# MLP down-projection in two passes over 1024 columns, 18 of 64 pairs of k-tiles with Strassen's seven block products

## The chip, the core and the metric

The kernel runs on one core of a Trainium2 chip. TensorE multiplies (its results go to PSUM, in eight banks of 128 x 512 float32 numbers), VectorE (DVE), ScalarE (ACT) and GpSimd (POOL) compute on SBUF, and SyncE (SP) issues most of the transfers from memory. Each engine works off its own instructions in a fixed order, and semaphores tie the engines together. The metric is the device time of one execution in microseconds: before the change a median of 2107.43 us over three runs (2106.3 to 2108.21).

## The reference

A trunk of two layers over 256 tokens of 2048 numbers, all in float32. Layer 0 mixes tokens with a state-space mixer, layer 1 with windowed attention; each is followed by an MLP of width 8192:

```python
def sqrelu_mlp(h, w_up, w_down):
    return jnp.square(jax.nn.relu(h @ w_up)) @ w_down
...
        h = h + sqrelu_mlp(rms_norm(h, mlp_norm[i]), mlp_w_up[i], mlp_w_down[i])
```

The change concerns the second product: 256 tokens x 8192 times 8192 x 2048, once per layer.

## The kernel before

Every float32 number that TensorE multiplies is split into a high part (`hi`, rounded to TensorE's fast format by a cast on ScalarE, line 667) and a low part (`lo`, the rest, by a subtract on VectorE, line 668). A product is then three matmuls: high x high, low x high, high x low.

Weights stream through three rings of buffers of 128 x 2048: `raw` (two buffers, loaded from memory on SP's queue, line 662), `hi` (three) and `lo` (three). `wnext` hands out the oldest loaded block and lets `wload` load one ahead. A raw buffer is free again when its subtract is done, a high or low buffer when the last matmul that reads it is done.

`mlp` first does the up-projection: 64 blocks of 128 hidden units, each with 16 matmuls of 512 columns (line 827) and 16 of 256 columns (line 829); the input lies in `act`, high and low part side by side. `up_post` adds, rectifies, scales and squares into `hT`, which holds all 8192 hidden units of the 256 tokens in float32.

Then comes the down-projection, 64 k-tiles of 128 hidden units. `split(kt)` (lines 871 and 872) makes the high and low part of that k-tile's activations, 256 columns, in a pool of three buffers that lies apart from `act`. `down` then does, for each of two token tiles, three runs of four matmuls of 512 columns (line 879): the four column blocks follow each other with the same stationary operand, and all eight banks collect over the whole 64 k-tiles. That is 24 matmuls per k-tile, 1536 per MLP. The last two k-tiles are held back and done bank by bank, so that `end` (line 909) adds each finished bank to the residual while TensorE goes on. After the first MLP `end` also prepares the next norm (a multiply on GpSimd, line 704, and squares on ScalarE, line 706); after the second it sends the output.

What order the instructions have on each engine is set by a scheduler when the program is built: it goes by dependences, by the order of the code and by its own timing model, and may move an instruction far ahead where its buffers allow it.

## Time and profile before

| what | us |
|---|---|
| median of three runs | 2107.43 |
| the profiled execution | 2104.89 |
| its span in the trace | 2103.1 |
| first down-projection, first to last matmul, from 752.5 | 348 |
| second down-projection, from 1750.9 | 348.2 |

The profile describes one execution. A row of a group names a line of the kernel, the engine, the operation, the operands (output, arrow, inputs), and then how many there were, their busy time together, and the mean of one in ns. A row of the timeline begins with the start and the length in us; rows of equal instructions are merged, with their count behind the x. The chain of waits follows the work that ended last back from the end. PE is TensorE's matmul, PEld its load of the stationary operand.

### The profile page before, as it was taken

Reading aid. Unit: us, or ns where it says so; the run is one execution under the profiler, and the core shown is the slowest. Engines: PE = TensorE matmul, PEld = TensorE weight load, DVE = VectorE, ACT = ScalarE, POOL = GpSimd, SP = SyncE. Lnnn points to the kernel's source line nnn. Section 1 sums busy time; section 2 is a strip of 40 time slices with the busy share of each in tenths; the row PEclk is TensorE's granted clock in tenths of the full one; section 3 lists DMA queues with packets and bytes.
Section 4 is the critical chain, followed back from the end, with each engine's and each line's share of the span. In section 5 each row is a group of like instructions: output and inputs, shape, how many; then the busy total and the mean of one; then the engine's idle time right before and its main releaser. Section 6 shows DMA issues by size and latency. Waiting matters only on the chain. (4 is left out here: it accounts for less than half of the span.)

```text
span 2103.1 us, 33054 instructions
## 1 busy us (share of the span) xinstructions
PE 2029.9 (97%) x13844; PEld 1712.2 (81%) x13844; DVE 1245.2 (59%) x1824; ACT 979.8 (47%) x1238; POOL 330.1 (16%) x248
## 2 busy tenths in 40 slices
PE   4989999899999999999999889999999999999999
PEld 4877778788888888888888667788888888888887
DVE  8899736755555554444556877565555555444444
ACT  5553645544444444344444556544444444443442
POOL 5988721200000000000012430100000000000000
PEclk9999999999999999999999999999999999999999
DMA  3224455455555555655554332455555555555554
GB/s 119 69 98 144 151 196 195 177 187 196 182 197 182 193 187 194 208 197 196 194 178 170 121 121 81 150 189 201 191 185 196 182 197 182 200 187 193 200 187 153
DMA packets 59685, 364.28 MB, mean 173 GB/s; under 512 B 6816, under 2 KB 9152, under 8 KB 19600
## 3 DMA queue, kind: packets, MB, share of 16 engines
q1 hardware_dynamic: 54144, 342.32, 46.4%
q10 hardware_dynamic: 5184, 19.49, 2.8%
q8 instruction: 108, 1.77, 0.3%
q14 instruction: 41, 0.34, 0.0%
q0 software_dynamic: 208, 0.36, 0.0%
HBM read 360.05 MB, written 2.10 MB: 172 GB/s over the span
## 5 line engine op out<-in xcount | busy, mean ns | idle before, releaser
L668 DVE TENSOR_TENSOR slot<-slot,slot 128x2048 fp32r<-128x2048 f32 (+1 forms) x321 | 714.6, 2229 | 737.3 <-ACT slot L667 730.2
L667 ACT CAST slot<-slot 128x2048 fp32r<-128x2048 f32 (+2 forms) x357 | 623.0, 1751 | 731.0 <-PE bank L879 377.7
L879 PE MATMUL bank<-slot,slot 128*128 128x512 f32 x3072 | 696.7, 389 | 0.0
L879 PEld LDWEIGHTS bank<-slot,slot 128*128 128x128 f32 x3072 | 576.6, 188 | 119.4
L827 PE MATMUL bank<-slot,slot 128*128 128x512 f32 x2048 | 492.0, 392 | 3.1 <-DVE ms L724 1.7
L827 PEld LDWEIGHTS bank<-slot,slot 128*128 128x128 f32 x2048 | 376.8, 189 | 76.6 <-DVE slot L716 2.1
L829 PEld LDWEIGHTS bank<-slot,slot 128*128 128x128 f32 x2048 | 263.1, 191 | 10.3
L829 PE MATMUL bank<-slot,slot 128*128 128x256 f32 x2048 | 266.2, 283 | 0.0
L686 PE MATMUL bank<-slot,slot 128*128 128x512 f32 x544 | 218.6, 403 | 6.2 <-ACT slot L667 4.9
L687 PE MATMUL bank<-slot,slot 128*128 128x512 f32 x544 | 214.9, 395 | 0.0
L688 PE MATMUL bank<-slot,slot 128*128 128x512 f32 x544 | 208.6, 396 | 6.3 <-POOL slot L668 6.1
L837 ACT ACTIVATE slot<-slot 128x256 f32<-128x256 f32 x128 | 52.9, 415 | 164.1 <-DVE slot L836 164.1
L686 PEld LDWEIGHTS bank<-slot,slot 128*128 128x128 f32 x544 | 103.5, 190 | 30.9 <-ACT slot L667 6.1
L688 PEld LDWEIGHTS bank<-slot,slot 128*128 128x128 f32 x544 | 102.0, 189 | 30.0 <-POOL slot L668 7.6
L687 PEld LDWEIGHTS bank<-slot,slot 128*128 128x128 f32 x544 | 103.5, 190 | 20.6 <-issue 0.5
L668 POOL TENSOR_TENSOR slot<-slot,slot 128x1024 fp32r<-128x1024 f32 (+2 forms) x36 | 101.1, 2819 | 103.4 <-ACT slot L667 98.2
L950 POOL DMA_DIRECT2D slot<-in_pos x1 | 0.8, 754 | 608.2 <-DVE slot L872 608.2
L532 DVE TENSOR_TENSOR bank<-bank,slot 128x256 f32<-128x256 f32 x126 | 54.4, 431 | 4.1
L836 DVE SCALAR_TENSOR_TENSOR slot<-slot 128x256 f32<-128x256 f32 x128 | 54.2, 425 | 4.2
L872 DVE TENSOR_TENSOR slot<-slot,slot 128x256 fp32r<-128x256 f32 x128 | 53.4, 418 | 4.0 <-ACT slot L871 4.0
L704 POOL TENSOR_TENSOR slot<-slot 128x512 f32<-128x512 f32 x16 | 28.0, 1758 | 172.7 <-DVE slot L1158 62.6
L871 ACT CAST slot<-slot 128x256 fp32r<-128x256 f32 x128 | 51.1, 400 | 7.9 <-PE bank L879 7.9
(217 smaller groups left out, 1390.8 us busy)
## 6 DMA issues: line engine op xcount, KB each, us to landing
slot<-in_wup SPq DMA_DIRECT2D x128, 1024.0 KB, 4.8
slot<-in_wdn SPq DMA_DIRECT2D x128, 1024.0 KB, 4.8
slot<-in_wqkv SPq DMA_DIRECT2D x20, 1024.0 KB, 4.9
slot<-in_wge ACTq DMA_DIRECT2D x32, 512.0 KB, 3.7
slot<-in_wgl SPq DMA_DIRECT2D x16, 1024.0 KB, 5.1
slot<-in_wo SPq DMA_DIRECT2D x16, 1024.0 KB, 5.0
slot<-in_bz SPq DMA_DIRECT2D x16, 336.0 KB, 3.7
slot<-in_cp SPq DMA_DIRECT2D x16, 256.0 KB, 2.6
```

The costliest lines, as they stand in the source:

```text
L532: yield v.tensor_mul(xy, lb, st[:, k - 1].rearrange("p r (o g) -> p r o g", o=1).broadcast_to([P, 2, 2, n]))
L667: self.nc.scalar.copy(hi[:, c], raw[:, c])
L668: (self.nc.gpsimd if e == "g" else self.nc.vector).tensor_sub(lo[:, c], raw[:, c], hi[:, c].bitcast(F32))
L686: pe.matmul(out, lhsT=xh, rhs=wh, start=first, stop=False)
L687: pe.matmul(out, lhsT=xl, rhs=wh, start=False, stop=False)
L688: pe.matmul(out, lhsT=xh, rhs=wl, start=False, stop=last)
L827: pe.matmul(bk, lhsT=wh[:, kt], rhs=act[:, kt].rearrange("p x c -> p (x c)"), start=(kt == 0), stop=False)
L829: pe.matmul(bk[:, :L], lhsT=wl[:, kt], rhs=act[:, kt, 0], start=False, stop=(kt == KT - 1))
L836: nc.vector.scalar_tensor_tensor(s, s, 0.0, rb, op0=ALU.max, op1=ALU.mult)
L837: nc.scalar.activation(hT(fb), s, AF.Square)
L872: nc.vector.tensor_sub(hl, hT(kt), hh.bitcast(F32))
L879: pe.matmul(bks[tt][cb], lhsT=x[:, ts], rhs=w[:, cb * 512:(cb + 1) * 512], start=(kt == 0 and w is wh and x is hh), stop=(kt == NK - 1 and ...
```

## The change

**Layout.** The down-weights are stored anew: a load of 128 x 2048 now holds two k-tiles (256 hidden units) by 1024 output columns, as four blocks of 512 columns in the order B12, B22, B11, B21 (row: which k-tile; column: which half of the 1024). It is still 1 MB, and there are still 64 per MLP.

**Two passes.** The down-projection goes over the 32 pairs of k-tiles twice, each time for 1024 of the 2048 columns. A pass collects in four banks, one for each token tile and column block. `split` now prepares a pair of k-tiles (512 columns), and does so in both passes.

**Strassen.** A plain pair is eight block products (two token tiles, two k-tiles, two column blocks), 24 matmuls. In 9 of the 32 pairs of a pass, every third one, seven products take their place, 21 matmuls (Winograd's form of Strassen's scheme). For these pairs `split` also makes four sums of activation blocks and their high and low parts; `wload_fast` splits three of the weight blocks as they are, then forms differences in place in the raw buffer, and splits all four results. So such a pair takes two high and two low buffers. Four more banks (`p1`, `q5`, `q6`, `q7`) collect over the Strassen pairs of a pass; `fold` adds them to the residual after the last of them.

**Buffers.** For the down-projection each ring gets one buffer more: a raw one at 49664 and a high and a low one in the area of `act`, at 23552 and 25600. The parts of the activations (`aform`) lie in the area of `act` too, at 27648 and 29696. In the first pass Strassen pairs are 2, 5, ... 26, in the second 0, 3, ... 24; with three raw buffers they all use the one at 49664.

**The end.** In the first MLP, the norm's preparation of the first 1024 columns is issued in the second pass already (pair 19).

In the order listings below, `slot_82` is the area of the old raw buffers, `slot_83` that of the new one, `slot_4069` that of the old high buffers, `slot_2733` and `slot_2734` that of the low ones, `slot_4067` (from 23552) that of `act` and now of `aform` and the new high and low buffer, `slot_313`, `slot_4602` and `slot_4603` are `hT`, `slot_7236` held the parts of the activations before, and `slot_79` is a small pool, now with the activation sums too.

First place: VectorE in the middle of the first pass of the first down-projection. Before, from the middle of the same down-projection:

```order
L872 TENSOR_TENSOR slot_7236<-slot_313,slot_7236 128x256
L668 TENSOR_TENSOR slot_2733<-slot_82,slot_4069 128x2048
L872 TENSOR_TENSOR slot_7236<-slot_313,slot_7236 128x256
L668 TENSOR_TENSOR slot_2734<-slot_82,slot_4069 128x2048
L872 TENSOR_TENSOR slot_7236<-slot_313,slot_7236 128x256
```

Now, 12 of the 14 instructions of one period of three pairs (a Strassen pair and two plain ones; the two left out are the first sum, L903, ahead of these rows, and one more low part, L909, behind them):

```order
L688 TENSOR_TENSOR slot_83<-slot_83 128x512
L904 TENSOR_TENSOR slot_79<-slot_79,slot_4602 128x128
L686 TENSOR_TENSOR slot_2734<-slot_83,slot_4069 128x1536
L905 TENSOR_TENSOR slot_79<-slot_79,slot_4602 128x128
L689 TENSOR_TENSOR slot_83<-slot_83 128x512
L690 TENSOR_TENSOR slot_83<-slot_83 128x1024
L672 TENSOR_TENSOR slot_4067<-slot_82,slot_4067 128x2048
L909 TENSOR_TENSOR slot_4067<-slot_313,slot_4067 128x512
L686 TENSOR_TENSOR slot_2734<-slot_83,slot_4069 128x2048
L672 TENSOR_TENSOR slot_2733<-slot_82,slot_4069 128x2048
L909 TENSOR_TENSOR slot_4067<-slot_313,slot_4067 128x512
L909 TENSOR_TENSOR slot_4067<-slot_79,slot_4067 128x512
```

Where a subtract of 2048 and one of 256 columns took turns, six of the 14 instructions now make sums and differences, and all low parts of activations are 512 columns wide. L688 to L690 are the differences of weight blocks, L903 to L905 the sums of activation blocks; the second subtract of the Strassen pair (L686 with 2048 columns), which gives up the raw buffer `slot_83`, stands between the two subtracts of plain pairs.

Second place: VectorE at the seam between the first MLP's up- and down-projection. Before:

```order
L668 TENSOR_TENSOR slot_2734<-slot_82,slot_4069 128x2048
L835 TENSOR_TENSOR slot_79<-bank,slot_79 128x256
L836 SCALAR_TENSOR_TENSOR slot_79<-slot_79 128x256
L668 TENSOR_TENSOR slot_2734<-slot_82,slot_4069 128x2048
L872 TENSOR_TENSOR slot_7236<-slot_313,slot_7236 128x256
L668 TENSOR_TENSOR slot_2733<-slot_82,slot_4069 128x2048
```

Now:

```order
L903 TENSOR_TENSOR slot_79<-slot_313 128x256
L904 TENSOR_TENSOR slot_79<-slot_79,slot_313 128x128
L686 TENSOR_TENSOR slot_2734<-slot_83,slot_4069 128x1536
L905 TENSOR_TENSOR slot_79<-slot_79,slot_313 128x128
L672 TENSOR_TENSOR slot_4067<-slot_82,slot_4067 128x2048
L689 TENSOR_TENSOR slot_83<-slot_83 128x512
L909 TENSOR_TENSOR slot_4067<-slot_313,slot_4067 128x512 x2
L858 TENSOR_TENSOR slot_79<-bank,slot_79 128x256
L909 TENSOR_TENSOR slot_4067<-slot_79,slot_4067 128x512
```

Before, the parts of the first activations (L872, into an area of their own) stood much earlier, among the first blocks of the up-projection. Now the first low part (L909) stands behind the subtracts of two weight blocks (L686, L672) and a difference (L689). At the same seam of the second MLP (`slot_9722` is the new raw buffer there, `slot_11474` is `hT`) it is this:

```order
L903 TENSOR_TENSOR slot_79<-slot_11474 128x256
L904 TENSOR_TENSOR slot_79<-slot_79,slot_11474 128x128
L686 TENSOR_TENSOR slot_2734<-slot_9722,slot_4069 128x1536
L905 TENSOR_TENSOR slot_79<-slot_79,slot_11474 128x128
L909 TENSOR_TENSOR slot_4067<-slot_11474,slot_4067 128x512 x2
L858 TENSOR_TENSOR slot_79<-bank,slot_79 128x256
L689 TENSOR_TENSOR slot_9722<-slot_9722 128x512
L909 TENSOR_TENSOR slot_4067<-slot_79,slot_4067 128x512
```

There no subtract of 2048 columns stands ahead of the first L909.

Third place: SP's queue around the GLU's loads, long ahead of the first MLP. Before:

```order
L562 DMA slot_241<-in_bz 128x672
L662 DMA slot_82<-in_wgl 128x2048 x2
L697 DMA slot_73<-in_gains 128x512 x2
L662 DMA slot_82<-in_wgl 128x2048 x6
L697 DMA slot_73<-in_gains 128x512
```

Now:

```order
L564 DMA slot_241<-in_bz 128x672
L666 DMA slot_82<-in_wgl 128x2048
L679 DMA slot_83<-in_wdn 128x2048
L666 DMA slot_82<-in_wgl 128x2048
L720 DMA slot_73<-in_gains 128x512 x2
L666 DMA slot_82<-in_wgl 128x2048 x6
L720 DMA slot_73<-in_gains 128x512
```

The first load for a Strassen pair stands behind the first GLU load, because its buffer is free so early. On TensorE the two down-projections have 1482 matmuls each where they had 1536; away from them, and from the transposes behind the first, the order of TensorE's instructions is as it was.

The diff, without the lines that only rename:

```diff
+WD = 20 + 16 + 64 + 64
+FAST = (range(2, 27, 3), range(0, 25, 3))
...
+            if len(self.wsrc) in self.wfast:
+                return self.wload_fast(src)
...
+    def wload_fast(self, src):
+
+        v = self.nc.vector
+        raw = self.wr[0].next()
+        self.nc.sync.dma_start(raw, src)
+        b = [raw[:, i * 512:(i + 1) * 512] for i in range(4)]
+        pair = raw[:, 1024:].rearrange("p (x c) -> p x c", x=2)
+        out = []
+        for x, n in (raw[:, 512:], 1536), (raw, 2048):
+            hi, lo = (r.next()[:, :n] for r in self.wr[1:])
+            self.nc.scalar.copy(hi, x)
+            v.tensor_sub(lo, x, hi.bitcast(F32))
+            if n < D:
+                v.tensor_sub(b[0], b[0], b[2])
+                v.tensor_sub(b[1], b[1], b[0])
+                v.tensor_sub(pair, pair, b[1].rearrange("p (o c) -> p o c", o=1).broadcast_to([P, 2, 512]))
+            out += [(hi, lo)]
+        self.wq.append(out)
...
-            t = pool.tile([P, L], F32, name="up_t")
+            t = pool.tile([P, 512], F32, name="u5")
+            t, s = t[:, :L], t[:, L:]
             nc.scalar.copy(t, bk[:, L:])
-            s = pool.tile([P, L], F32, name="up_s")
...
-        def split(kt):
-            hh = pool.tile([P, L], F32R, name="hh", bufs=3)
-            hl = pool.tile([P, L], F32R, name="hl", bufs=3)
-            nc.scalar.copy(hh, hT(kt))
-            nc.vector.tensor_sub(hl, hT(kt), hh.bitcast(F32))
-            return hh, hl
-
-        def down(kt, tt, hh, hl, wh, wl, cbs=range(4)):
-            ts = slice(tt * P, (tt + 1) * P)
-            for x, w in ((hh, wh), (hl, wh), (hh, wl)):
-                for cb in cbs:
-                    pe.matmul(bks[tt][cb], lhsT=x[:, ts], rhs=w[:, cb * 512:(cb + 1) * 512],
-                              start=(kt == 0 and w is wh and x is hh), stop=(kt == NK - 1 and w is wl))
+        def split(kp, fast, tail=False):
+            h = hTs[0][:, 2 * kp:2 * kp + 2] if kp < 16 else hTs[kp // 8 - 1][:, kp % 8 * 2:kp % 8 * 2 + 2]
+            h = h.rearrange("p k c -> p (k c)")
+            a = (atail if tail else aform)[kp % 2]
+            n = a.shape[1] // 2
+            o = [(a[:, :512], a[:, n:n + 512], h)]
+            if fast:
+                s = pool.tile([P, 512], F32, name="u5")
+                q = h.rearrange("p (x c) -> p x c", x=4)
+                t = s.rearrange("p (x c) -> p x c", x=4)
+                v.tensor_add(t[:, 0:2], q[:, 0:4:3], q[:, 1:2].broadcast_to([P, 2, P]))
+                v.tensor_add(t[:, 2], t[:, 1], q[:, 0])
+                v.tensor_add(t[:, 3], t[:, 2], q[:, 2])
+                o.append((a[:, 512:n], a[:, n + 512:], s))
+            for hi, lo, x in o:
+                nc.scalar.copy(hi, x)
+                v.tensor_sub(lo, x, hi.bitcast(F32))
+            return a[:, :n], a[:, n:]
+        def mm(bk, a, j, w, c, stop=False):
+            j, c = slice(j * P, (j + 1) * P), slice(c * 512, (c + 1) * 512)
+            for x, y in ((0, 0), (1, 0), (0, 1)):
+                pe.matmul(bank(bk), lhsT=a[x][:, j], rhs=w[y][:, c], start=bk not in begun, stop=stop and y == 1)
+                begun.add(bk)
...
+        FORMS = (("p1", 0, 0, 1), ("x1", 2, 0, 2), ("x2", 7, 0, 0), ("q5", 5, 1, 0), ("q6", 6, 1, 1), ("q7", 4, 1, 2), ("x3", 3, 1, 3))
+        LATE = FORMS[:1] + FORMS[3:6] + FORMS[1:3] + FORMS[6:]
+
+        def fast(a, w, first, end):
+            for bk, j, g, c in LATE if first else FORMS:
+                mm(bk, a, j, w[g], c, stop=end and bk[0] != "x")
+
+        def plain(a, w, bk, stop=False):
+            t, j = divmod(bk, 2)
+            bk = "x%d" % (bk + 1)
+            for i in range(2):
+                mm(bk, a, 2 * i + t, w, (2, 3)[i] if j == 0 else i, stop=stop and i == 1)
...
+        def fold():
+            c, u, w = (self.tmp.tile([P, 512], F32, name=n) for n in ("hg", "sq", "gain"))
+            nc.scalar.copy(c, bks["p1"])
+            v.tensor_sub(u, bks["q6"], c)
+            v.tensor_add(rs(0, 0), rs(0, 0), c)
+            v.tensor_add(w, u, bks["q5"])
+            v.tensor_sub(rs(0, 1), rs(0, 1), w)
+            v.tensor_add(u, u, bks["q7"])
+            v.tensor_add(rs(1, 0), rs(1, 0), u)
+            v.tensor_add(u, u, bks["q5"])
+            v.tensor_add(rs(1, 1), rs(1, 1), u)
...
+        def end(half, t, j):
+            cb = half * 2 + j
+            cs = slice(cb * 512, (cb + 1) * 512)
+            v.tensor_add(self.resid[:, t, cs], self.resid[:, t, cs], bks["x%d" % (2 * t + j + 1)])
...
-        pend = []
-        for kt in range(NK):
-            hh, hl = nx
-            wh, wl = self.wnext() if kt else w0
-            if kt + 1 < NK:
-                nx = split(kt + 1)
-            if kt == NK // 2 + 4 and not last:
...
+        aform += [ar.get("af#%d" % i, [2048], F32R, at=27648 + 2048 * i) for i in range(2)]
+        more = [ar.get("wx#%d" % at, [2048], dt, at=at) for at, dt in ((49664, F32), (23552, F32R), (25600, F32R))]
+        for r, t in zip(self.wr, more):
+            r.tiles.append(t)
+        nx = split(0, 0 in FAST[0])
+        for half in range(2):
+            bks, begun = {}, set()
+            pend = []
+            for kp in range(NK):
+                a = nx
+                w = self.wnext() if half or kp else w0
+                if half and kp == NK - 4:
+                    for r in self.wr:
+                        r.tiles.pop()
+                        r.i = min(r.i, len(r.tiles) - 1)
+                    ar.free("wx")
+                    atail += [ar.get("at#%d" % i, [1024], F32R, at=49664 + 1024 * i) for i in range(2)]
+                if kp + 1 < NK:
+                    nx = split(kp + 1, kp + 1 in FAST[half], half and kp + 1 >= NK - 2)
+                elif not half:
+                    nx = split(0, 0 in FAST[1])
+                if half and kp == 19 and not last:
+                    ar.free("hT#0")
+                    hx = ar.get("hx", [2, 4, 512], at=31744)
+                    gains = ar.get("hg", [D], at=35840)
+                    nc.sync.dma_start(gains, self.d["gains"][nxt])
+                    self.ss = self.small.tile([P, 2, 4], F32, name="ss")
+                    for t in range(2):
+                        for cb in range(2):
+                            scaled(t, cb)
+                if kp in FAST[half]:
+                    fast(a, w, not begun, kp == FAST[half][-1])
+                    if kp == FAST[half][-1]:
+                        fold()
+                elif kp < NK - 1 - half:
+                    for b in range(4):
+                        plain(a, w, b)
+                else:
+                    pend.append((a, w))
+            if half:
+                ar.free("hT", "af")
+                if not last:
+                    self.act = ar.get("act", [KT, 2, L], F32R, at=23552)
+            n = half and not last
+            for t in range(2):
+                for p in pend[:n]:
+                    for j in range(2):
+                        plain(*p, 2 * t + j)
+                for j in range(2):
+                    for p in pend[n:]:
+                        plain(*p, 2 * t + j, stop=p is pend[-1])
+                    end(half, t, j)
...
+        self.wfast = {n - 1 - 32 * h - kp for n in (64, 64 + WD) for h in range(2) for kp in FAST[h]}
...
-    r["wdn"] = c(mlp_w_down).reshape(2, FF // P, P, D)
+    w = mlp_w_down.reshape(2, FF // P // 2, 2, P, 2, 2, 512).transpose(0, 4, 1, 3, 2, 5, 6).reshape(2, 2, FF // P // 2, P, 4, 512)
+    r["wdn"] = c(w[:, :, :, :, [1, 3, 0, 2]]).reshape(2, FF // P, P, D)
```

51 lines of the change are left out of this document (18 added, 33 removed).

## The prediction

> **What bounds the kernel now.** I read the page first, then the chain of waits, the windows, the groups by form and last the timeline of the down-projection. On the page TensorE is busy for almost the whole span, and the chain of waits that ended last shows the second down-projection as one unbroken piece:
>
> ```profile
> PE 2029.9 (97%) x13844; PEld 1712.2 (81%) x13844; DVE 1245.2 (59%) x1824; ACT 979.8 (47%) x1238; POOL 330.1 (16%) x248
> ...
> 1750.91 348.20 PE bank L879 x1536
> ```
>
> 1536 matmuls in 348.20 us are 226.7 ns each, with no wait between them. The windows view over the first down-projection (columns: length, busy us with instruction counts for PE, PEld, DVE, ACT, POOL, then granted clock, DMA share, GB/s) says what the others have left:
>
> ```profile
> 752.00:1100.00 348.00, 348.00 (x1539) 288.36 (x1539) 174.79 (x166) 143.04 (x137) 7.93 (x9) 1.00 0.56 197
> ```
>
> VectorE works half the time, ScalarE 41%, DMA engines 56%. So a matmul taken away here is worth its 226.7 ns, as long as the operands still arrive in time. The timeline shows the feeding of one k-tile, every 5.44 us:
>
> ```profile
> 898.75 1.91 ACT L667 CAST slot<-slot 128x2048 fp32r<-128x2048 f32 x1 [3.23 <-PE bank L879]
> 900.69 2.29 DVE L668 TENSOR_TENSOR slot<-slot,slot 128x2048 fp32r<-128x2048 f32 x1 [2.81 <-ACT slot L667]
> 902.90 0.42 DVE L872 TENSOR_TENSOR slot<-slot,slot 128x256 fp32r<-128x256 f32 x1
> 903.01 0.33 SPq L662 DMA_DIRECT2D slot<-in_wdn  x1
> ```
>
> The cast waits for TensorE to give up a high tile, the subtract follows 0.03 us behind it, and the next load is issued 0.03 us after the subtract has given up the raw buffer. The L872 subtract starts 0.08 us before the listed end of the one ahead of it: independent VectorE operations overlap by that much.
>
> **What goes.** A plain pair of k-tiles by 1024 columns costs 8 products of 3 matmuls, a Strassen pair 7 of 3. 18 pairs in each of two MLPs remove 18 x 3 x 2 = 108 matmuls: 108 x 0.2267 = **24.5 us**, if the rate stays. One thing could alter the rate: the four column blocks that shared a stationary operand are gone, the stationary changes with each matmul. The up-projection already works so:
>
> ```profile
> 1500.41 3.65 PE bank L827 x16
> ...
> 1501.63 2.43 PE L827 MATMUL bank<-slot,slot 128*128 128x512 f32 x10
> ```
>
> Sixteen from the start of a block take 228.1 ns each, which over 2964 matmuls would cost 4.2 us. But ten from its middle take (2.43 - 0.39) / 9 = 226.7 (0.39 is the last one's own length): the excess belongs to the change from narrow matmuls. I take 0, with 4.2 as the upper end.
>
> **What is added, in steady state.** The pattern repeats every three pairs, one Strassen and two plain: 21 + 24 + 24 = 69 matmuls, 15.64 us. The prices:
>
> ```profile
> L668 DVE TENSOR_TENSOR slot<-slot,slot 128x2048 fp32r<-128x2048 f32 x285 | 654.0, 2295 | 720.8 <-ACT slot L667 715.9 <-PE bank L688 4.9
> L667 ACT CAST slot<-slot 128x2048 fp32r<-128x2048 f32 x293 | 559.5, 1910 | 669.7 <-PE bank L879 377.7 <-PE bank L827 193.7 <-DMA slot<-in_wgl 27.3
> L533 DVE TENSOR_TENSOR slot<-bank,slot 128x128 f32<-128x128 f32 x126 | 36.6, 291 | 4.2
> L872 DVE TENSOR_TENSOR slot<-slot,slot 128x256 fp32r<-128x256 f32 x128 | 53.4, 418 | 4.0 <-ACT slot L871 4.0
> L909 DVE TENSOR_TENSOR slot<-slot,bank 128x512 f32<-128x512 f32 x16 | 10.7, 684 | 8.2 <-PE bank L879 8.1
> L667 ACT CAST slot<-slot 128x512 fp32r<-128x512 f32 x4 | 2.3, 618 | 1.0 <-DVE slot L668 1.0
> ```
>
> Between 256 and 2048 columns a VectorE operation costs 1.05 ns per column, so 1.22 us at 1024 and 1.76 at 1536 are my estimates; a cast of 1536 is 1.48 the same way. VectorE per period: weights of the Strassen pair 1.76 + 2.30, block differences 0.68 + 0.68 + 1.22, activation sums 0.42 + 0.29 + 0.29, their low parts 2 x 0.68; two plain pairs 2 x (2.30 + 0.68). That is **15.0 us** in 14 operations without any overlap, 13.9 with 0.08 each: 89 to 96% of 15.64. ScalarE: 1.48 + 3 x 1.91 + 4 x 0.62 = 9.7. Loads: three, 14.4 us even one after the other (4.8 each, below). So all of it hides, VectorE narrowly. If that cover were gone, the excess over 15.64 would be paid in each of 36 periods.
>
> The narrowest place is the raw buffer that every Strassen pair uses again, three pairs later. Its round: load D, cast 1.48, subtract 1.76, one activation sum 0.29, differences 0.68 and 1.22, then (the second cast runs beside them) a plain subtract 2.30, a low part 0.68 and the second subtract 2.30, as VectorE's order has them. That is D + 10.7, or D + 10.3 with the overlaps. D is read here:
>
> ```profile
> slot<-in_wdn SPq DMA_DIRECT2D x128, 1024.0 KB, 4.8
> DMA to landing us min/median/max: 4.7/4.8/5.5
> ...
> L662 SPq DMA_DIRECT2D slot<-in_wdn x2: 328/328/328, 765.2 to 767.7; - x2
> DMA to landing us min/median/max: 4.7/4.8/4.8
> ...
> L662 SPq DMA_DIRECT2D slot<-in_wgl x2: 328/356/383, 354.6 to 356.9; - x2
> DMA to landing us min/median/max: 7.7/7.8/7.9
> ```
>
> With 4.8 the round is 15.1 to 15.5, inside 15.64 by 0.1 to 0.5 us. In the new order three buffers are released within some 5 us, so loads go out about 2.7 us apart; the pair at 765.2 and 767.7 had that distance and landed in 4.8 all the same. The pair of 7.8 stood behind another load issued 0.4 us ahead. I take D = 4.8 to 5 and no cost.
>
> The fold of the four extra banks (eight VectorE operations, 5.5 us, once per pass) falls on plain pairs, where VectorE needs 3.0 of 5.44 us; its banks are wanted again only after five pairs. Evictions at the end of a pass (0.68 each) are covered by the next pass, which begins with the other four banks: 12 matmuls, 2.7 us. Both 0; uncovered, 5 us a pass. The four early scalings of the first MLP put four GpSimd multiplies beside the subtracts, and those two disturb each other:
>
> ```profile
> L668 DVE TENSOR_TENSOR slot<-slot,slot x321: 1211/2292/5580, 164.9 to 2083.8; 128x2048 fp32r<-128x2048 f32 x143, 128x1024 fp32r<-128x1024 f32 x18
> L668 DVE TENSOR_TENSOR slot<-slot,slot 128x1024 fp32r<-128x1024 f32 x36 | 60.7, 1699 | 16.5 <-ACT slot L667 14.3 <-PE bank L829 2.1
> 1094.23 5.05 POOL L704 TENSOR_TENSOR slot<-slot,slot 128x512 f32<-128x512 f32 x4 [75.31 <-DVE slot L909]
> ```
>
> 1024 columns take 1211 ns alone and 1699 on average in stages with GpSimd at work, 40% more; over 5.05 us that is 2 us late, once. Half of it finds slack: **1.0 us** (0 to 2). The same scalings leave half as much for the tail, worth 0 to 1 us; I take 0.
>
> **What is moved.** One load of down-weights stands on SP's queue between the first two GLU loads:
>
> ```profile
> 255.29 19.18 SPq L662 DMA_DIRECT2D slot<-in_wgl  x2
> 274.64 0.80 SPq L697 DMA_DIRECT2D slot<-in_gains  x2
> 298.94 0.33 SPq L662 DMA_DIRECT2D slot<-in_wgl  x1
> ```
>
> The second GLU load was issued at 274.5, the third only at 298.9; behind the moved load 24 us are free, so 0 (4.8 if they were not). VectorE's first difference goes with it, far ahead of need.
>
> **The start of each down-projection** is a new wait. The activation operands, and a fourth high and low tile, now lie where the up-projection's input was, which is read until its last matmul; before, they lay elsewhere and were ready early. At the seam now:
>
> ```profile
> 750.63 2.08 PE L829 MATMUL bank<-slot,slot 128*128 128x256 f32 x16
> 752.55 5.63 PE L879 MATMUL bank<-slot,slot 128*128 128x512 f32 x24
> ...
> 752.80 2.29 DVE L668 TENSOR_TENSOR slot<-slot,slot 128x2048 fp32r<-128x2048 f32 x1 [2.48 <-ACT slot L667]
> ```
>
> VectorE takes up its next weight tile 0.25 us after the seam. By its new order the first low part stands behind it: in the first MLP 1536 columns, an activation sum, 2048 columns, a difference, then the low part, 1.76 + 0.29 + 2.30 + 0.68 + 0.68 = 5.7; in the second 1.76 + 0.29 + 0.68 = 2.7. Only four matmuls (0.9 us) do without low parts. Idle: 0.25 + 5.7 - 0.9 less overlaps = 4.7, and 1.9: **6.6 us**. Lower end: one cast of 0.62 per MLP, 1.2 in all; upper end 12, if the second goes like the first. Such a gap can also cost clock:
>
> ```profile
> 395.77 1.12 PE L713 MATMUL bank<-ident,slot 128*128 128x128 f32 x4 [3.95 <-POOL slot L704]
> 395.00:400.00 5.00, 4.23 (x14) 3.54 (x15) 4.58 (x18) 1.41 (x4) 2.00 (x2) 0.66 0.33 136
> ...
> 1103.66 0.50 PE L686 MATMUL bank<-slot,slot 128*128 128x512 f32 x1 [1.01 <-ACT slot L716]
> 1098.00:1106.00 8.00, 6.99 (x43) 5.96 (x42) 7.10 (x18) 5.04 (x13) 6.28 (x6) 1.00 0.00 0
> ```
>
> After 3.95 us of idleness the granted clock was 0.66 over 5 us (0.34 x 5 = 1.7 us lost); after 1.01 it stayed 1.00. The first start lies near the longer gap but is cut by four matmuls: 0.8 us, between 0 and 1.7. The Trainium skill ("TensorE: Matmul & The Clock Gate", section "Why this matters for your kernels") says that idle gaps over about 3 us bring the half clock back; the trace agrees, and by that rule alone the first start would cost the full 1.7, a sum later by 0.9.
>
> **Sum.** 24.5 - 6.6 - 1.0 - 0.8 = 16.1 us. The profiled execution took 2104.89 (span 2103.1): 2088.8. The median of the three runs, 2107.43, lies 2.5 above it: **2091 us**.
>
> **Rivals.**
> - The raw buffer's round decides (slower). For it: releases in a bunch, and loads that took 7.8 in bunches. Against it: the pair at 765.2. There are 8 rounds between Strassen pairs in each of 4 passes, 32. The gain is used up when a round takes 15.64 + 16.1 / 32 = 16.1 us, so from D = 5.4 to 5.8 on. With D = 6.3, halfway to 7.8, a round takes 16.6 to 17.0: 1.2 x 32 = 38 us, less 16.1 gained, about 2129 us.
> - VectorE becomes the bound: its waits on its own results keep the operations from overlapping and add some 0.07 us each, 15.0 + 1.0 = 16.0. That is 0.36 x 36 = 13 us given back: 2104 us. For it: the sums and differences depend on each other. Against it: most subtracts are independent.
> - The starts cost only their casts, 1.2, and nothing else is lost: 24.5 - 1.2 = 23.3, 2084 us. For it: TensorE's last up matmuls free parts of that area early. Against it: the order on VectorE.
> - The change not doing what it says is left out: the order has 1482 matmuls in each down-projection for 1536.
>
> **How the numbers follow.** Forecast 0.70, raw buffer 0.10, VectorE bound 0.13, free starts 0.07. The forecast's own bounds (rate up to 4.2, starts 1.2 to 12, scaling, clock) reach from 2084 to 2100. The range goes to 2103.5, up to the VectorE case, and leaves the slower one out: 2084 to 2103.5. A measurement of this kernel tells no less than 0.2%, 4.2 us, from no change. Faster: 0.70 + 0.07 + a little under half of 0.13 = 0.83; same 0.07; slower 0.10.
>
> **What would show it.** 1482 matmuls of the down-projection at 226.7 ns, 336 us, with idle time only in their first 10 us; VectorE about 90% busy while Strassen pairs run; load landings at 4.8 to 5. Wrong, if TensorE waits for VectorE in each period, if the casts of Strassen pairs wait for their load, or if matmuls run at 228 ns.

## The result, and the profile after

The changed kernel takes 2090.7 us (median, 2089.6 to 2094.4), the kernel before 2107.3: a ratio of 0.9924, 95% interval 0.991 to 0.9938, about 16 us less. The prediction was 2091. The profiled execution, the longest of the four, took 2094.37 (span 2092.6).

The page of the changed kernel: 108 matmuls fewer, 22 us less of TensorE, and VectorE up from 59 to 71%.

```profile
PE 2007.8 (96%) x13736; PEld 1692.1 (81%) x13736; DVE 1496.1 (71%) x2144; ACT 1083.2 (52%) x1314; POOL 335.3 (16%) x248
```

Its windows, 100 us in the middle of a first pass (columns as in the prediction). TensorE never stops, VectorE works 90.85 of 100 us:

```profile
800.00:900.00 100.00, 100.00 (x443) 82.79 (x442) 90.85 (x88) 60.72 (x53) 0.00 (x0) 1.00 0.54 198
```

Its chain of waits for the down-projections. Before, one row held all 1536 matmuls; now the first MLP's is in pieces, and the second's is whole from 1753 us on, 335.63 / 1478 = 227.1 ns each with the change of pass and the end in it:

```profile
760.64 231.84 PE bank L915 x1013
1000.92 62.86 PE bank L915 x276
1064.21 4.57 PE bank L915 x20
1070.14 31.78 PE bank L915 x140
...
1753.06 335.63 PE bank L915 x1478
```

What breaks it is seen in the timeline at the first start:

```profile
754.57 1.89 ACT L671 CAST slot<-slot 128x2048 fp32r<-128x2048 f32 x1
...
755.22 1.76 DVE L686 TENSOR_TENSOR slot<-slot,slot 128x1536 fp32r<-128x1536 f32 x1 [0.22 <-PE bank L852]
...
756.36 1.14 ACT L908 CAST slot<-slot 128x512 fp32r<-128x512 f32 x2
...
757.03 1.20 PE L915 MATMUL bank<-slot,slot 128*128 128x512 f32 x4 [1.38 <-ACT slot L908]
757.09 2.29 DVE L672 TENSOR_TENSOR slot<-slot,slot 128x2048 fp32r<-128x2048 f32 x1
...
759.29 0.68 DVE L689 TENSOR_TENSOR slot<-slot 128x512 f32<-128x512 f32 x1
759.90 1.29 DVE L909 TENSOR_TENSOR slot<-slot,slot 128x512 fp32r<-128x512 f32 x2
```

and, by the windows, in the 4 us behind it, at a granted clock of 0.57:

```profile
761.00:765.00 4.00, 4.00 (x12) 3.13 (x11) 4.00 (x11) 0.46 (x2) 0.00 (x0) 0.57 0.61 238
```

Four matmuls start when the first cast (L908) is done, which on ScalarE stands behind the cast of a weight tile (L671); the fifth waits for the first low part (L909), which stands behind a whole weight tile on VectorE, and starts at 760.64. The other place is in the second pass of the first MLP:

```profile
988.50 9.61 POOL L727 TENSOR_TENSOR slot<-slot,slot 128x512 f32<-128x512 f32 x4 [587.52 <-DVE slot L690]
...
988.78 3.17 DVE L672 TENSOR_TENSOR slot<-slot,slot 128x2048 fp32r<-128x2048 f32 x1 [0.40 <-ACT slot L671]
...
991.88 1.78 DVE L909 TENSOR_TENSOR slot<-slot,slot 128x512 fp32r<-128x512 f32 x1
...
993.58 3.38 DVE L686 TENSOR_TENSOR slot<-slot,slot 128x2048 fp32r<-128x2048 f32 x1
...
996.89 3.37 DVE L672 TENSOR_TENSOR slot<-slot,slot 128x2048 fp32r<-128x2048 f32 x1
...
997.02 2.11 PE L915 MATMUL bank<-slot,slot 128*128 128x512 f32 x8 [0.70 <-DVE slot L686]
```

The four GpSimd multiplies of the early scaling take 9.61 us together, and four VectorE operations beside them take 0.88, 1.10, 1.09 and 1.08 us more than their 2.29 and 0.68. One by one, the multiplies took 1.30 us and then, in the timeline:

```profile
989.76 3.35 POOL L727 TENSOR_TENSOR slot<-slot,slot 128x512 f32<-128x512 f32 x1
...
993.07 1.75 POOL L727 TENSOR_TENSOR slot<-slot,slot 128x512 f32<-128x512 f32 x1
...
994.78 3.33 POOL L727 TENSOR_TENSOR slot<-slot,slot 128x512 f32<-128x512 f32 x1
```

Set side by side, the rows show the two engines taking turns. Each of the four VectorE operations ends its usual 2.29 or 0.68 us, less 0.13 to 0.15, behind the end of the multiply that was running when it started. Each of these three multiplies ends 1.15 or 1.16 us behind the end of the VectorE operation that was running. So each waited until the other had all but finished.

I added up, over all matmuls of the down-projections, how much later than 226.6 ns behind the one ahead each starts, leaving out differences under 0.02 us: 0 before, 11.1 us now: 4.1 of waits at the first start and 1.7 of half clock behind it, 3.0 beside the multiplies, 1.5 at the second start, and 0.8 at the changes of pass and the end. 24.5 - 11.1 = 13.4 us, within the interval. The two profiled executions differ by 10.5 us; the other 3 lie ahead of the first down-projection, since the up-projection's last matmul started at 755.4 us here and at 752.4 before, which is scatter as far as the other profiles tell (see the moved load below). This sum, called TensorE's loss below, is what the experiments take apart. Their ratios are to the kernel before, which was timed again beside each of them (medians of 2105.8 to 2106.5 us).

### The profile page after: what moved, and what is told of

Its sections match the earlier page's. It is cut to its first block, busy times and chain, and to the rows that moved or that the text cites. A ratio compares the mean times of both kernels' runs of the same rounds, so it can differ in the third digit from the quotient of the medians.

```text
span 2092.6 us, 33181 instructions
## 1 busy us (share of the span) xinstructions
PE 2007.8 (96%) x13736; PEld 1692.1 (81%) x13736; DVE 1496.1 (71%) x2144; ACT 1083.2 (52%) x1314; POOL 335.3 (16%) x248
## 4 chain that ended last, share of the span: by engine, by line
PE 72%; DVE 5%; DMA 3%; ACT 2%; issue 1%; POOL 0%; SPq 0%; ACTq 0%; DVEq 0%
PE bank L915 32%; PE bank L850 22%; PE bank L852 12%; DVE slot L672 2%; PE bank L709 2%; PE bank L710 1%; PE bank L711 1%; ACT slot L671 1%; DMA slot<-in_wqkv 1%; DMA slot<-in_wo 1%; ACT slot L1136 1%; PE bank L1155 1%; DMA slot<-in_wup 1%; PE bank L1146 1%; DVE slot L1121 0%
## 5 line engine op out<-in xcount | busy, mean ns | idle before, releaser
L672 DVE TENSOR_TENSOR slot<-slot,slot 128x2048 fp32r<-128x2048 f32 (+1 forms) x285 | 633.9, 2227 | 426.6 <-ACT slot L671 423.2
L671 ACT CAST slot<-slot 128x2048 fp32r<-128x2048 f32 (+2 forms) x321 | 554.4, 1733 | 485.2 <-PE bank L850 192.0
L915 PE MATMUL bank<-slot,slot 128*128 128x512 f32 x2136 | 496.2, 390 | 7.4 <-DVE slot L909 5.3
L850 PE MATMUL bank<-slot,slot 128*128 128x512 f32 x2048 | 492.8, 392 | 2.9 <-DVE ms L747 1.5
L915 PEld LDWEIGHTS bank<-slot,slot 128*128 128x128 f32 x2136 | 401.4, 188 | 93.5 <-DVE slot L909 7.4
L850 PEld LDWEIGHTS bank<-slot,slot 128*128 128x128 f32 x2048 | 377.4, 189 | 76.7 <-DVE slot L739 2.1
L852 PEld LDWEIGHTS bank<-slot,slot 128*128 128x128 f32 x2048 | 263.1, 191 | 10.4
L709 PE MATMUL bank<-slot,slot 128*128 128x512 f32 x544 | 217.9, 402 | 6.9 <-ACT slot L671 6.3
L711 PE MATMUL bank<-slot,slot 128*128 128x512 f32 x544 | 208.3, 396 | 7.7 <-POOL slot L672 7.5
L710 PE MATMUL bank<-slot,slot 128*128 128x512 f32 x544 | 214.2, 394 | 0.0
L915 PE MATMUL bank<-slot 128*128 128x512 f32 x828 | 195.8, 389 | 0.0
L915 PEld LDWEIGHTS bank<-slot 128*128 128x128 f32 x828 | 155.3, 188 | 32.3
L686 DVE TENSOR_TENSOR slot<-slot,slot 128x1536 fp32r<-128x1536 f32 x72 | 146.7, 2037 | 19.0 <-ACT slot L685 18.2
L685 ACT CAST slot<-slot 128x1536 fp32r<-128x1536 f32 x72 | 122.3, 1698 | 41.7 <-DMA slot<-in_wdn 28.3
L908 ACT CAST slot<-slot 128x512 fp32r<-128x512 f32 x164 | 97.5, 616 | 82.9 <-PE bank L915 78.4
L709 PEld LDWEIGHTS bank<-slot,slot 128*128 128x128 f32 x544 | 103.2, 190 | 31.0 <-ACT slot L671 7.5
L711 PEld LDWEIGHTS bank<-slot,slot 128*128 128x128 f32 x544 | 101.9, 189 | 31.4 <-POOL slot L672 9.4
L909 DVE TENSOR_TENSOR slot<-slot,slot 128x512 fp32r<-128x512 f32 x164 | 110.7, 693 | 15.7 <-ACT slot L908 15.7
L710 PEld LDWEIGHTS bank<-slot,slot 128*128 128x128 f32 x544 | 103.3, 190 | 20.7 <-issue 0.7
L672 POOL TENSOR_TENSOR slot<-slot,slot 128x1024 fp32r<-128x1024 f32 (+2 forms) x36 | 100.5, 2803 | 104.6 <-ACT slot L671 100.9
```

What stands on the lines that cost most here:

```text
L671: self.nc.scalar.copy(hi[:, c], raw[:, c])
L672: (self.nc.gpsimd if e == "g" else self.nc.vector).tensor_sub(lo[:, c], raw[:, c], hi[:, c].bitcast(F32))
L685: self.nc.scalar.copy(hi, x)
L686: v.tensor_sub(lo, x, hi.bitcast(F32))
L709: pe.matmul(out, lhsT=xh, rhs=wh, start=first, stop=False)
L710: pe.matmul(out, lhsT=xl, rhs=wh, start=False, stop=False)
```

## Experiments

**Two passes without Strassen pairs.**

```diff
-FAST = (range(2, 27, 3), range(0, 25, 3))
+FAST = ((), ())
```

> The two passes over 1024 columns without any Strassen pair: 1536 matmuls per down-projection again, operand layout, buffers, early scaling and moved load as in the changed kernel. Theory (the gain is 108 matmuls of 226.6 ns, 24.5 us, and two passes cost only the waits that the changed kernel shows: 4.1 at the first start, 1.7 of half clock, 1.5 at the second start, 3.0 around the GpSimd multiplies, 10 in all): 4 to 11 us slower than before, about 2111 to 2118 us, and 20 to 25 us slower than the changed kernel; without a Strassen pair at the start the first waits may be shorter, which is the low end. Rival (narrow stationary operands, changed with each matmul, cost rate: up to 228.1 ns): 1536 matmuls twice at 228 ns, 4 us more than that. Rival (the two passes gain something by themselves, and Strassen's pairs bring less than 24.5): not slower than before.

Measured: 2114.75 us, ratio 1.0042 (1.0028 to 1.0055), 9 us slower than before; TensorE's loss 9.8 us, nearly all at the two starts. The pairs themselves are thus worth 1.0042 - 0.9924 = 0.0118, 25 us, give or take 4: the 24.5 of their 108 matmuls. The excess lies at the starts, not in the pace, which is 226.7 ns where nothing waits, as before: no cost of rate.

**The early scaling issued late.** Two tries, the multiplies alone and then the whole block with the load of the gains:

```diff
-                    for t in range(2):
-                        for cb in range(2):
-                            scaled(t, cb)
...
             elif half:
+                scaled(t, j)
                 scaled(t, cb)
```

```diff
-                if half and kp == 19 and not last:
+                if half and kp == 26 and not last:
```

> The changed kernel with the four GpSimd multiplies of the first 1024 columns at the end of the first MLP's second pass, as before, and not beside the subtracts at its pair 19. Theory (those multiplies slow VectorE's subtracts from 2.29 to 3.2-3.4 us and cost the 3.0 us of waits seen at 997 to 1001 us): these waits are gone, and the tail after the down-projection is 0 to 3 us longer, since eight squares and multiplies instead of four stand there; in all 0 to 3 us faster than the changed kernel. Rival (the wait at 997 us comes from the period of a Strassen pair itself, VectorE being at its bound, and the multiplies only happen to stand there): a wait of 1 to 3 us stays in the second pass.

> The changed kernel with the whole block of the early scaling (the area's release, the load of the gains and the four GpSimd multiplies) at pair 26 of the first MLP's second pass instead of pair 19. In the run with late scaling only the multiplies were moved in the program, and GpSimd, which has nothing queued ahead of them, ran them at the same place all the same (986 us), as soon as the gains had landed; this one moves what they wait for. Theory (the multiplies slow VectorE's subtracts from 2.29 to 3.2-3.4 us, and TensorE waits 3.0 us for these): no wait over 0.4 us between 914 and 1060 us, subtracts of 2048 there at 2.29, and at the new place, where no Strassen pair is left and VectorE has 3.0 of 5.4 us to do, at most 1 us; 2 to 3 us less than the changed kernel. Rival (the pair at 997 us waits for another reason, such as the period itself): a wait of 1 to 3 us stays between 985 and 1003 us with all subtracts at 2.29.

Measured: 2090.05 us, 0.9928 (0.9915 to 0.994), and 2089.86, 0.9929 (0.9917 to 0.9942): no difference from the changed kernel. Neither moved what it meant to move. The timelines of the first and of the second:

```profile
986.29 9.60 POOL L727 TENSOR_TENSOR slot<-slot,slot 128x512 f32<-128x512 f32 x4 [586.42 <-DVE slot L690]
```

```profile
987.84 9.67 POOL L727 TENSOR_TENSOR slot<-slot,slot 128x512 f32<-128x512 f32 x4 [587.71 <-DMA slot<-in_gains]
```

GpSimd had been idle for 586 us and ran the multiplies as soon as their data was there, 0.13 us behind the landing of the gains (986.16 and 987.71 us; L690, which the first row names, ended in the same moment); the load of the gains, too, went out as soon as the area that it goes to was read for the last time. So these two runs say nothing on the cause of the 3.0 us.

**The first pair's activation parts in an area of their own.** It is free during the up-projection; afterwards it becomes the third raw buffer. The Strassen pairs of the first pass move by two. A second kernel also issues the early multiplies at pair 27 (last two lines).

```diff
-FAST = (range(2, 27, 3), range(0, 25, 3))
+FAST = (range(4, 29, 3), range(0, 25, 3))
...
-        nx = split(0, 0 in FAST[0])
+        nx = split(0, 0 in FAST[0], a=ar.get("a0", [1024], F32R, at=49664))
...
+                if not half and kp == 3:
+                    ar.free("a0")
+                    self.wr[0].tiles.append(ar.get("wx#49664", [2048], at=49664))
...
+                if half and kp == 27 and not last:
                     for t in range(2):
```

> The changed kernel with the first pair's activation parts in an area that is free during the up-projection (the third raw buffer joins only at pair 3), and the Strassen pairs of the first pass at 4, 7, ... 28 instead of 2, 5, ... 26 (still nine). Theory (both starts are late because the first activation parts may be written only after the up-projection's last matmul, and then stand behind a whole weight tile on VectorE): no idle time over 0.5 us in the first 10 us of either down-projection, no half clock at the first; 4.1 + 1.7 + 1.5 = 7.3 us less than the changed kernel, 5 to 8 by the median, about 2083 to 2086 us. Rival (the starts are late because the weight tiles are, TensorE having to wait for high and low parts of weights in any case): the idle time stays within 1.5 us of what it was, gain under 3 us.

> The activation parts of the first pair in an area of their own (as in the kernel before this one) and the early GpSimd multiplies put behind the last Strassen pair of the second pass (pair 27 instead of 19), where VectorE has slack. Theory (the waits at the starts and around the multiplies are all that the changed kernel loses): 7.3 + 3.0 = 10.3 us less than the changed kernel, 7 to 11 by the median, about 2080 to 2084 us, and faster than the kernel before by 23 to 28 us. Rival (the multiplies slow whatever stands beside them, pair 27 included): the 3 us of waits appear there, 5 to 8 us less than the changed kernel.

Measured: 2089.07 us, 0.992 (0.9907 to 0.9934), and 2088.21, 0.9919 (0.9906 to 0.9933). Both starts are free of waits, as the theory said, and yet only 1 or 2 us are gained, no more than the scatter: TensorE's loss is still 7.9 and 8.6 us. The multiplies stayed where they were, and new waits came up at the changes of pass. The timeline of the first of the two, second MLP:

```profile
1908.97 0.68 DVE L944 TENSOR_TENSOR slot<-slot 128x512 f32<-128x512 f32 x1
...
1913.38 0.68 DVE L953 TENSOR_TENSOR slot<-slot,bank 128x512 f32<-128x512 f32 x1
...
1917.98 0.68 DVE L953 TENSOR_TENSOR slot<-slot,bank 128x512 f32<-128x512 f32 x1
1918.58 0.68 DVE L948 TENSOR_TENSOR slot<-slot 128x512 f32<-128x512 f32 x1
...
1919.18 2.28 DVE L672 TENSOR_TENSOR slot<-slot,slot 128x2048 fp32r<-128x2048 f32 x1
...
1921.38 0.68 DVE L909 TENSOR_TENSOR slot<-slot,slot 128x512 fp32r<-128x512 f32 x1
...
1922.12 2.12 PE L915 MATMUL bank<-slot 128*128 128x512 f32 x8 [1.67 <-DVE slot L909]
```

The fold (L944 to L948), the evictions (L953) and the next Strassen pair's work now fall together, since the last Strassen pair of the first pass stands at 28 and not at 26. VectorE, covered in the middle of a pass, is late at its end; the next kernels test this.

**The same with five plain pairs between the passes,** and then with the whole scaling block at pair 26 as well:

```diff
-FAST = (range(4, 29, 3), range(0, 25, 3))
+FAST = (range(3, 28, 3), range(1, 26, 3))
```

> As the kernel with the first pair's activation parts apart, whose starts had no wait, but which lost 2.1 and 2.9 us again at the changes of pass; the Strassen pairs stand one pair earlier in the first pass (3, 6, ... 27) and one later in the second (1, 4, ... 25), so that five plain pairs instead of three lie between the last of one pass, whose fold adds 5.5 us of VectorE work, and the first of the next. Theory (fold, evictions and the next Strassen weights came too close together on VectorE): waits at the changes of pass under 1 us each, starts without wait; the 3.0 us beside the GpSimd multiplies stay; 7.3 - 1 = 6 us less than the changed kernel, 4 to 8 by the median. Rival (a change of pass costs 2 to 3 us with these pairs too, because the third raw buffer joins late or the loads do): 2 to 3 us less than the changed kernel.

> The two edits of this call together: the first pair's activation parts apart with Strassen pairs at 3 ... 27 and 1 ... 25, and the early scaling with its load at pair 26. Theory (starts 7.3 and multiplies 3.0 us are all that TensorE waits for in the changed kernel's down-projections, 11.1 by the trace): 8 to 10 us less than the changed kernel, about 0.988 of the kernel before, 2081 us; TensorE's waits in the four passes under 2 us in all. Rival (what is saved here is given back elsewhere, as in the run with the parts apart): under 5 us less.

Measured: 2085.34 us, 0.9904 (0.9889 to 0.9919), and 2085.02, 0.9907 (0.9893 to 0.992); TensorE's loss 6.0 and 4.7 us, 4 to 6 us less time than the changed kernel. The first did as expected: the waits at the changes of pass are under 1 us, and of what is left over half is one wait beside the multiplies. In its timeline:

```profile
986.88 10.74 POOL L727 TENSOR_TENSOR slot<-slot,slot 128x512 f32<-128x512 f32 x4 [587.44 <-DMA slot<-in_gains]
...
998.23 3.29 PE L915 MATMUL bank<-slot 128*128 128x512 f32 x7 [2.87 <-DVE slot L909]
```

The second missed its 8 to 10 us, because its block came no later (987 us again).

**The multiplies held back by data.** The area of gains and scaled columns now holds the activations of pairs 16 to 27 instead of 0 to 11; all else as in the last kernel.

```diff
-enumerate(((32, 31744), (16, 39936), (16, 44032)))
+enumerate(((16, 39936), (16, 44032), (24, 31744), (8, 37888)))
...
-                    ar.free("hT#0")
+                    ar.free("hT#2")
```

> As the kernel with both edits, but the GpSimd multiplies are now held back by data: in the two runs that moved them in the program they ran at 986-988 us all the same, as soon as the area of the first 32 activation k-tiles was read and the gains had landed in it. Here that area holds the k-tiles of pairs 16 to 27 (the other activations lie elsewhere, nothing else differs), so that gains and multiplies can come only behind pair 27's split, where no Strassen weights are left. Theory (the multiplies cost the waits at 993-1000 us, 3.0 to 3.3 us and sometimes a half clock behind them): no wait over 0.4 us and no subtract of 2048 over 2.4 us between 985 and 1003 us; the multiplies at about 1060 us stretch VectorE there, which has 3.0 of 5.4 us to do, at most 1 us of waits; TensorE's waits in the four passes under 3 us in all (11.1 in the changed kernel), 3 us less than the kernel with both edits, 8 to 11 less than the changed kernel, 2080 to 2083 us. Rival (the wait belongs to the period at that place): 2 us or more of waits stay at 993-1000 us.

Measured: 2081.94 us, 0.9883 (0.9866 to 0.99), as expected, faster than the kernel before and 8 to 9 us below the changed one. TensorE's loss is 1.6 us in 2964 matmuls. The timeline now has the multiplies at 1066 us, and in the second pass VectorE's subtracts at 2.29:

```profile
1066.45 8.66 POOL L727 TENSOR_TENSOR slot<-slot,slot 128x512 f32<-128x512 f32 x4 [101.12 <-DMA slot<-in_gains]
```

```profile
985.04 2.29 DVE L672 TENSOR_TENSOR slot<-slot,slot 128x2048 fp32r<-128x2048 f32 x1
...
989.08 2.29 DVE L686 TENSOR_TENSOR slot<-slot,slot 128x2048 fp32r<-128x2048 f32 x1 [0.19 <-ACT slot L685]
...
991.39 2.29 DVE L672 TENSOR_TENSOR slot<-slot,slot 128x2048 fp32r<-128x2048 f32 x1
```

At their new place the multiplies stretch VectorE's operations again:

```profile
1068.92 3.33 DVE L672 TENSOR_TENSOR slot<-slot,slot 128x2048 fp32r<-128x2048 f32 x1
1072.17 1.77 DVE L911 TENSOR_TENSOR slot<-slot,slot 128x512 fp32r<-128x512 f32 x1
...
1074.36 2.90 DVE L672 TENSOR_TENSOR slot<-slot,slot 128x2048 fp32r<-128x2048 f32 x1 [0.41 <-ACT slot L671]
```

There, with no Strassen pair near, TensorE does not wait for them: its matmuls from 1065 to 1077 us follow each other without a gap. Against the kernel with both edits only the areas of the activations differ in the program, and through them the time of the gains' load and the multiplies (some small VectorE work for the next layer went the other way, from 1058 to 1084 us to 967 to 995, which leaves VectorE more to do there, not less); TensorE's loss fell by 3.0 us. The cause is the multiplies, not the period.

**Another order on VectorE.** The parts apart as above, with the pairs of the changed kernel and the third raw buffer joining two pairs earlier:

```diff
-FAST = (range(3, 28, 3), range(1, 26, 3))
+FAST = (range(2, 27, 3), range(0, 25, 3))
...
-                if not half and kp == 3:
+                if not half and kp == 1:
```

> The kernel with the parts apart, its Strassen pairs at 2, 5, ... 26 and 0, 3, ... 24 as in the changed kernel and the third raw buffer two pairs earlier. All work is the same, but on VectorE a plain tile's subtract of 2048 columns now stands between the steps of the Strassen differences, and another between them and the second subtract: behind the landing come the cast 1.48, then 1.76 + 0.29 + 2.30 + 0.68 + 0.29 + 0.68 + 1.22 + 2.30 + 0.68 + 2.30, together 14.0 or 13.1 with 0.09 us of overlap each, for the 10.3 to 10.7 of the changed kernel. Theory (the round of the raw buffer decides as soon as it is longer than the period of 15.64): 4.8 + 13.1 to 14.0 = 17.9 to 18.8 us per period, 2.3 to 3.1 us of waits in each of 32 rounds, 70 to 100 us, less 6 saved at the starts: 2155 to 2185 us. Rival (only VectorE's sum of work counts, which is the same): 2084 to 2090 us.

Measured: 2174.03 us, 1.0321 (1.0299 to 1.0343), in the expected range, though not as expected in detail: the order is different in the first passes alone, which take 211 and 212 us for 168, and the second passes have the good order (their last 716 matmuls run unbroken in the second MLP). A round of the first pass, from its timeline: the Strassen load (L679) goes out when the second subtract (L686) of the Strassen pair before has given up the buffer, and 18.17 us later the next one does.

```profile
837.33 0.33 SPq L679 DMA_DIRECT2D slot<-in_wdn  x1
...
842.22 0.69 DVE L688 TENSOR_TENSOR slot<-slot 128x512 f32<-128x512 f32 x1
...
843.77 1.75 DVE L686 TENSOR_TENSOR slot<-slot,slot 128x1536 fp32r<-128x1536 f32 x1
...
845.64 2.29 DVE L672 TENSOR_TENSOR slot<-slot,slot 128x2048 fp32r<-128x2048 f32 x1
...
849.25 1.22 DVE L690 TENSOR_TENSOR slot<-slot 128x1024 f32<-128x1024 f32 x1
...
850.38 2.28 DVE L672 TENSOR_TENSOR slot<-slot,slot 128x2048 fp32r<-128x2048 f32 x1
...
853.18 2.28 DVE L686 TENSOR_TENSOR slot<-slot,slot 128x2048 fp32r<-128x2048 f32 x1
...
855.50 0.33 SPq L679 DMA_DIRECT2D slot<-in_wdn  x1
```

4.9 to the landing and 13.3 of use; two plain subtracts (L672) stand inside the chain where the good order has one. Other rounds of this pass took 17.0 to 22.1; the eight average 19.5 us, and what lengthened the longer ones was not taken apart. In the changed kernel the same two loads go out 15.64 us apart:

```profile
836.53 0.33 SPq L679 DMA_DIRECT2D slot<-in_wdn  x1
...
852.17 0.33 SPq L679 DMA_DIRECT2D slot<-in_wdn  x1
```

The work is the same in both, and VectorE works only 68.9 of the 100 us from 800 on, so its sum is not what decides; the round of the raw buffer is: VectorE's first difference (L688) waited 32.6 us in all for these loads, 4.7 in the changed kernel. Eight rounds of 19.5 instead of 15.64 us are 31 of the 43 us that this pass lost.

**Two raw buffers.**

```diff
-        more = [... for at, dt in ((49664, F32), (23552, F32R), (25600, F32R))]
+        more = [... for at, dt in ((23552, F32R), (25600, F32R))]
...
-        for r, t in zip(self.wr, more):
+        for r, t in zip(self.wr[1:], more):
...
```

> The changed kernel without the third raw buffer (two, as before; the fourth high and low tile stay). A Strassen pair holds its buffer for load and use some 15.3 us, a plain pair at least 4.8 + 1.9 + 2.3 = 9.0: 33.3 us per period in two buffers, 16.7 where TensorE has 15.64. Theory (the raw buffers are what the period has least to spare of): at least 1.0 us of waits per period, 36 us, up to 2 us with what each buffer waits for a high tile, 72: 2127 to 2163 us. Rival (VectorE, not the buffers, sets the pace): within 5 us of the changed kernel.

Measured: 2174.74 us, 1.0334 (1.0307 to 1.0361), 84 us above the changed kernel and beyond the 36 to 72 expected. Four periods between 796 and 868 us took 72.1, 18.0 each. The casts of Strassen pairs waited for their load, in the groups:

```profile
L685 ACT CAST slot<-slot 128x1536 fp32r<-128x1536 f32 x72 | 122.1, 1696 | 127.9 <-DMA slot<-in_wdn 82.0
```

The direction holds (the buffers, not VectorE, which is busy 79% of 800 to 900 us); the bound of 16.7 was too low by 1.3 us a period. That it left out what a tile waits for with all operands in order is likely, but not shown.

**Every second pair.**

```diff
-FAST = (range(2, 27, 3), range(0, 25, 3))
+FAST = (range(2, 27, 2), range(0, 25, 2))
```

> The changed kernel with every second pair as a Strassen pair (13 in each pass, 26 of 64 pairs of an MLP), 48 more matmuls removed, 10.9 us. In a period of two pairs TensorE has 45 matmuls, 10.2 us, VectorE 9.0 + 3.0 = 12.0 us in 12 operations, 11.1 with overlaps. Theory (VectorE's work per period, with overlaps, is the limit that a third of the pairs just keeps, 13.9 of 15.64): 0.9 to 1.8 us of waits in each of 48 periods, 43 to 86 us, less 10.9: slower than the changed kernel by 30 to 75 us, 2120 to 2165 us. Rival (a matmul taken away is worth its 0.227 us here too, VectorE hides what is added): 10 us faster than the changed kernel.

Measured: 2182.29 us, 1.0357 (1.0335 to 1.0379): slower by more than expected, 92 us above the changed kernel. A period of two pairs takes 12.7 us (eight from 791 to 892 us) for TensorE's 10.2. Windows and groups of this kernel:

```profile
800.00:900.00 100.00, 87.35 (x358) 64.30 (x357) 88.63 (x96) 53.56 (x48) 0.00 (x0) 1.00 0.46 168
```

```profile
L671 ACT CAST slot<-slot 128x2048 fp32r<-128x2048 f32 (+2 forms) x305 | 524.0, 1725 | 516.9 <-PE bank L850 189.0 <-DMA slot<-in_wdn 106.8 <-DMA slot<-in_wgl 31.2
```

VectorE is no fuller than in the changed kernel (88.6 to 90.9), and plain casts waited 107 us for their loads, which from 800 to 900 us took 6.1 to land (median) where the changed kernel's took 4.9. So here, too, it is not VectorE's sum alone; which link of load, cast and subtract sets 12.7 is left open.

**More VectorE work.** An add of 512 columns at each plain pair:

```diff
+            if not fast:
+                g = self.tmp.tile([P, 512], F32, name="gain")
+                v.tensor_add(g, h, h)
```

> The changed kernel with one more VectorE add of 512 columns (0.68 us, its result unused) at each plain pair, two in each period of three pairs. VectorE's period grows from 15.0 to 16.4 us without overlaps, from 13.9 to 15.1 with 0.08 us each, where TensorE's is 15.64. Theory (overlaps hold and VectorE is covered; a period does not pay): no wait in the middle of a pass, 0 to 8 us more in all, where VectorE is late anyway (starts, multiplies, changes of pass). Rival (VectorE is at its bound, its real period 15.5 or more): every period pays, 0.7 x 36 = 25 us or more.

Measured: 2104.55 us, 0.9993 (0.9985 to 1.0002), 14 us above the changed kernel, between theory and rival, and it tests neither. The windows show that the adds did not go where they were meant to:

```profile
800.00:900.00 100.00, 100.00 (x443) 82.84 (x442) 90.98 (x90) 60.32 (x52) 0.00 (x0) 1.00 0.57 210
```

90 VectorE instructions for 88, where 13 more belong: needing activations alone, the adds ran during the up-projection and in bunches at the starts and changes of pass. There TensorE's loss grew by 10 us (in the timeline, a wait at a change of pass that the changed kernel has not):

```profile
934.78 1.42 PE L918 MATMUL bank<-slot,slot 128*128 128x512 f32 x5 [2.20 <-DVE slot L909]
```

The two profiled executions differ by 10.5 us (2104.91 and 2094.37), so these 10 are nearly all of it; the medians differ by 14, since the changed kernel's profiled execution was 3.7 us longer than its median. How much VectorE work a period could still take was not measured.

## Why the prediction was right, step by step

- **108 matmuls, 24.5 us, no change of rate:** right. They run at 226.7 ns where nothing waits, and the kernel without Strassen pairs puts their worth at 25 us.
- **Steady state hidden:** right. No wait over 0.4 us in the middle of a pass but the two beside the multiplies (which the prediction's sign, idle time in the first 10 us only, had not allowed for), and VectorE busy 90.85% where 89 to 96 were worked out. The raw buffer's round, 15.1 to 15.5 by the prediction, fits: the one that begins with the load at 836.53 took 4.9 us to the landing and 10.7 to the release, and in the latter VectorE waited 0.5 us for casts. The rival that it decides was a close one: another order on VectorE, with one plain subtract more in the chain, cost 89 us against the kernel with the parts apart and five plain pairs between the passes (2174.03 to 2085.34).
- **A sign that was badly chosen:** the casts of Strassen pairs do wait for their load, 28.3 us in all in the changed kernel's groups, and TensorE loses nothing by it from 800 to 900 us:

```profile
L685 ACT CAST slot<-slot 128x1536 fp32r<-128x1536 f32 x72 | 122.3, 1698 | 41.7 <-DMA slot<-in_wdn 28.3
```

- **Starts, 4.7 and 1.9, 6.6 in all:** 4.1 and 1.5 by the trace, for the reason given: with the parts elsewhere both are 0, also with the Strassen pairs left at 2 and 0 (the kernel with another order on VectorE). But the way from there to the time led over the changes of pass (a gain of 1 to 2 us at first, 4 to 6 once the pairs were moved).
- **Half clock 0.8 (0 to 1.7):** 1.7, the upper end.
- **Early scaling 1.0 (0 to 2):** the term that was mis-sized. It was 3.0. The prediction let both engines go on side by side, VectorE 40% slower for the 5.05 us that the four multiplies take in the tail of the kernel before. Instead they took turns, which made it 9.6 us. "Half of it finds slack" was wrong too: 4.2 us of delay on VectorE, 3.0 on TensorE.
- **Changes of pass and fold, 0:** 0.8 by the trace, and 0 was lucky: with the first pass's Strassen pairs two later, the same work cost some 5 us.
- **Tail, 0 (0 to 1):** from the last matmul of the first down-projection to the first of the second it is 648.8 us for 649.8, a difference within the scatter (647.2 to 650.0 in seven of the other kernels).
- **Moved load, 0:** right, as far as the scatter lets it be seen. The kernels that have the third raw buffer from the start have a load of down-weights among the GLU's, the others have not. The up-projection's last matmul started at 751.4 to 755.4 us in the six profiles with it (mean 753.6), at 750.2 to 756.1 in the seven others (753.3), and at 752.4 in the kernel before.
- Losses of 8.4 were predicted and 11.1 measured in the profiled execution; by the medians 16.6 us were gained for 16.1 predicted. The difference is within what such a measurement tells. That the median came within 0.3 us of the forecast is luck in part: the starts were put 1.0 us too high, the scaling, the half clock and the changes of pass together 3.7 too low.

## What to carry to other kernels

An engine that is 90% busy in the middle of a loop can be covered there and still be late wherever the loop starts, ends, or meets a neighbour; cost those places one by one. Where a buffer is loaded, changed in place and released, write its round down in the order in which the engine executes it: an order with one more instruction of 2.3 us inside cost 89 us, more than all the matmuls saved. In four kernels here, an instruction on an idle engine ran when its data was there, whatever its place in the program: to move it, move the data that it waits for.

## What was not expected of the hardware

- **GpSimd beside VectorE.** A GpSimd multiply of 512 columns that takes 1.26 us in the tail of the kernel before took 1.30 to 3.35, 2.4 on average, beside VectorE's subtracts, and each lengthened one VectorE operation by 0.9 to 1.1 us. The two engines did not share the time but took turns, an instruction at a time, with 0.1 us of overlap.
- **Half clock after short waits.** Waits of 1.4 and 2.6 us split by four matmuls brought 6 to 8 matmuls at 427 ns in each of four profiles. A wait of 2.0 us beside the multiplies brought them in two of seven profiles, one of 3.0 in one of two. So the length of a wait does not settle it. The Trainium skill ("TensorE: Matmul & The Clock Gate", Part 1) says that the activity window of 3.4 us is free-running and does not start with the kernel; the scatter agrees with that, though these runs do not show the window itself.
